# First weights of the output projection loaded and split under the branches' merge, and the gate block summed two column tiles sooner

## Chip, cores, metric

One core of a Trainium2 chip. The metric is the device time of one execution in microseconds (us); several executions give a median. Engine names are those of the profile: PE multiplies matrices (PEld loads its weights), DVE is the vector engine, ACT the scalar engine, POOL is GpSimd, SP is the queue that issues nearly all transfers.

## What is computed

One layer on 640 tokens (128 context, 512 latent) of width 1024. The change lies in the middle of it, where the two branches are projected, merged by gates, and projected once more:

```python
ga, gb = jnp.split(gates, 2, axis=-1)
m = jax.nn.sigmoid(ga) * y_a + jax.nn.sigmoid(gb) * y_b
return m @ w_out, ...
...
x = x + gt1 * rms_norm(y, norm_gains[1])
```

Here `y_a = o @ w_br_a` and `y_b = (...) @ w_br_b` are the branches' projections (512 to 1024 columns each), and `gt1` is one 1024-wide block of `mod = silu(c) @ w_mod + b_mod`, the "gate block" of the title.

## The kernel before

Every float32 operand is split into a high and a low part (`split`, L50: ACT casts the high part, line L57; DVE subtracts it, line L58), and each product is three matmuls (`mm3`, lines L83 to L85). Weights stream from memory into raw buffers (`wr`), are split into `wh` and `wl`, and go to PE as the stationary operand. PSUM tiles of the projections are named `d` and have three buffers.

The order of work on each engine comes from a scheduler that takes the program in the order in which it is written, with priorities. An engine takes its instructions strictly in that order, and so does the SP queue: a transfer that waits holds up those behind it.

The stages that matter here, in order:

- Gate projections: `gate_th(i)` loads a weight tile, multiplies by the layer's input `hT` (two tiles `hT0` and `hT1` of 20 KB a partition), ACT takes the tanh (L735), and the result goes to memory as `thd`. Between them stand the last short convolution (`short(3)`, its product with the third projection on DVE at L724, its result stored as `ybd`, L725) and the sums of two other blocks of `mod` (`cm_rows`: matmuls on L208 and L209, then a round trip through memory into `sc2`, which DVE waits for at L249).
- Merge: for each of 8 column tiles `j`, load `w_br[j]` and two `thd` tiles (`bth`), four half projections of 12 matmuls (branch b, then branch a), and DVE and ACT form the merged tile as `mh[:, j]` and `ml[:, j]`. The input `y_b` is first read back from `ybd` in one transfer of 1280 KB (tile `ybr`, L972) and split into `ybh` and `ybl`; `y_a` is split from `zf` into `yah` and `yal`. Raw weights come from the pool `bp` with five buffers, which the gate block's `w_mod` tiles share.
- Gate block: `row_job` (L196) adds each of 8 `w_mod` tiles into two accumulators `gacc` on DVE (16 operations of 128x1024), one tile per column tile `j`. After the eighth, each accumulator is split (`cph`, `cpl`), summed over partitions by PE (L208, L209), and multiplied into `gt1` (L225).
- Output projection: `w_out` comes in eight tiles of 512 KB through two raw buffers, is split into the pool `wo` (eight buffers each for `woh` and `wol`), and PE forms `acc` for each token tile: `some(range(3), 0)` for the first three, then `prod`. This stage's PE order is written out by hand.

Pools are stacked from both ends of SBUF. What a pool places where a closed pool lay must wait until the old tiles have been read for the last time. The right-hand pool `hp2` is opened after the pools of `hT` and of the convolutions' tiles are closed, and covers part of where `hT1` lay.

Of the kernel before, what the change touches and what calls it, by code (L numbers as in the profile page):

```python
# [9 lines left out]
F32 = mybir.dt.float32  # L10
# [8 lines left out]
P = 128  # L19
D = 1024  # L20
# [3 lines left out]
TOK = CTX + LAT  # L24
# [13 lines left out]
class Kernel:  # L38
# [700 lines left out]
    def run(self):  # L739
        nc, tc, I, O = self.nc, self.tc, self.I, self.O  # L740
        pool = lambda st, name, bufs=1, **kw: st.enter_context(
            tc.tile_pool(name=name, bufs=bufs, **({} if kw.get("space") == DRAM else {"reuse_waits": "tile"}), **kw))
        stack = lambda *a, **kw: (lambda st: (st, pool(st, *a, **kw)))(ExitStack())
# [8 lines left out]
        hst, hp = stack("hp", side="right")  # L752
# [134 lines left out]
        def scan(p):  # L887
            with tc.high_priority(offset=300000):
# [26 lines left out]
        rows2 = lambda p: [p.tile([P, D], F32, name="gacc", tag="gacc", bufs=2) for _ in range(2)]  # L915
        raws = lambda p, n: lambda: p.tile([P, D], F32, name="wr", tag="wr", bufs=n)
        fill = itertools.chain(*(self.row_job(blk, rows2(mb), raws(mb, 4), self.cm_rows(cm[n], mb, ma, parts))
                                 for blk, n in ((3, "sh2"), (4, "sc2"))))
# [28 lines left out]
        for _ in fill:  # L947
# [11 lines left out]
        fd = lambda: self.psd.tile([P, 512], F32, name="d", tag="d")  # L959
        hst, hp = stack("hp2", side="right")  # L960
        mst, mp = stack("mp", side="right")
        gst, gp = stack("gp", side="right")
        b0st, bp0 = stack("bp0")
        bst, bp = stack("bp")
        self.rpool, self.nraw = bp, 5
        gt1 = gp.tile([P, 2, D], F32, name="gt1")
        fill = self.row_job(2, rows2(bp0), raws(bp, 5), self.gate_rows(gt1, 1, bp0.tile([P, D], F32, name="grow"), fd,
                                                                lambda acc: self.split(acc, [P, D], "cp", bp0, 1, urgent=False)))
        mh = mp.tile([P, KT, TOK], F32R, name="mh")
        ml = mp.tile([P, KT, TOK], F32R, name="ml")  # L970
        ybr = bp.tile([P, 4, TOK], F32, name="ybr")
        nc.sync.dma_start(out=ybr, in_=self.ybd.rearrange("i p t -> p i t"))  # L972
        yb = self.split(ybr, [P, 4, TOK], "yb", bp, 1)
        ya = self.split(self.zf, [P, 4, TOK], "ya", bp, 1)
        for j in range(KT):
            wb = self.load_w(I["w_br"][j], [P, 8, P])
            th = []
            for n in range(2):
                t_ = bp0.tile([P, TOK], F32, name="bth", tag="bth", bufs=4)
                nc.sync.dma_start(out=t_, in_=self.thd[2 * j + n])  # L980
                th.append(t_)
            for n, y in ((1, yb), (0, ya)):
                for h in range(2):
                    s = slice(h * HALF, (h + 1) * HALF)
                    ps = self.gemm_cm([w_[:, 4 * n:4 * n + 4, :] for w_ in wb], y, h, 4)
                    with self.urgent():
                        nc.vector.scalar_tensor_tensor(out=th[n][:, s], in0=th[n][:, s], scalar=1.0, in1=ps,
                                                       op0=ALU.add, op1=ALU.mult)
            next(fill, None)
            m = th[1]  # L990
            with self.urgent():
                nc.vector.tensor_tensor(out=m, in0=th[0], in1=th[1], op=ALU.add)
                nc.scalar.copy(out=mh[:, j, :], in_=m)
                nc.vector.tensor_tensor(out=ml[:, j, :], in0=m, in1=mh[:, j, :].bitcast(F32), op=ALU.subtract)
# [2 lines left out]
            pass  # L997
        bst.close()
        b0st.close()
        self.rpool, self.nraw = self.wpool, 2  # L1000

        wst2, wf = stack("wf", 2)
        pools = itertools.cycle((wf, self.wpool))
        h2 = [mh, ml]
        yst, bp = stack("yp", side="right")
        wost, wo = stack("wo")
# [4 lines left out]
        def load_o(src):  # L1013
            raw = self.rpool.tile([P, 2, 512], F32, name="wr", tag="wr", bufs=self.nraw)
            nc.sync.dma_start(out=raw, in_=src)
            return self.split(raw, [P, 2, 512], "wo", wo, 8)
        ws = [[load_o(I["w_out"][h, kk]) for kk in range(4)] for h in range(2)]
        ys = {}
        zx, xs = zp.tile([P, 4 * TOK], F32, name="zf"), {}
        quad = lambda: hp.tile([P, 4, TOK], F32, name="hq", tag="hq", bufs=2)  # L1020
        f = [quad(), quad()]

        def prod(t, h):
# [220 lines left out]
        with tc.manual_schedule(engines={mybir.EngineType.PE}):  # L1244
# [23 lines left out]
            for i, j in enumerate(rest):  # L1268
# [3 lines left out]
                if last:  # L1272
# [10 lines left out]
        fill = self.row_job(5, rows2(fq), raws(self.rpool, 2), self.gate_rows(gt2, 3, fq.tile([P, D], F32, name="grow2"), fd,  # L1283
                                                                      lambda acc: self.split(acc, [P, D], "w", next(pools), urgent=False)))
# [3 lines left out]
        def load_f(src):  # L1288
            raw = self.rpool.tile([P, 2, 512], F32, name="wr", tag="wr", bufs=self.nraw)
            nc.sync.dma_start(out=raw, in_=src)  # L1290
            return self.split(raw, [P, 2, 512], "w", next(pools))
# [22 lines left out]
        for kk in order:  # L1314
            split_act(kk)
            w = load_f(I["w_ffn_out"][0, kk])
# [10 lines left out]
        for kk in order[:-TAIL]:  # L1327
            if kk < NK - 6:
                split_act(kk)
            w = load_f(I["w_ffn_out"][1, kk])  # L1330
            for t in range(NT):
                part(acc[t], w, kk, t, order)
        ws = []
# [98 lines left out]
```

## Time and profile before

| what | value |
|---|---|
| median of 3 runs | 1089.17 us (1086.23 to 1091.02) |
| profiled execution, its own time | 1085.44 us |
| span of the profiled execution | 1083.7 us |
| PE busy | 1019.8 us, 94% of the span |
| DVE busy | 836.9 us, 77% |
| mean granted PE clock | 0.981 |

The span is what the profile shows of that execution; its own time also holds what lies around the span (1.7 us). Busy is time in which the engine executed. Matmuls are pipelined, so a matmul's duration in a row is longer than its step from start to start.

### The profile page before, as it was taken

To read this page: it belongs to the slowest core of one execution; us is meant where nothing else is said; L and a number is where in the kernel's file an instruction comes from. 1 tells how busy PE (TensorE), PEld (TensorE's weight loads), DVE (VectorE), ACT (ScalarE), POOL (GpSimd) and SP (SyncE) were. 2 spreads that over 40 slices of the span, in tenths; PEclk is the share of its full clock that TensorE was granted. 3 is DMA by queue.
4 is the path that set the end of the run, shared out by engine and by line. 5 is a ranking of instruction groups with operands and counts; after the bars stand their busy time and mean duration, and the time that the engine had idled before them with its cause. 6 is when DMAs were issued, how large, how long until landed. Compare 5 with 4: busy or idle time off the path is not lost.

```text
span 1083.7 us, 19694 instructions
## 1 busy us (share of the span) xinstructions
PE 1019.8 (94%) x7729; PEld 925.9 (85%) x7729; DVE 836.9 (77%) x1698; ACT 483.2 (45%) x927; POOL 141.9 (13%) x168
## 2 busy tenths in 40 slices
PE   6999988988988989999998998999999999999997
PEld 3699987878887788899996887999999999788885
DVE  5767997897898888895895789888777775975336
ACT  5568436415525323434223476444445444624321
POOL 2215321153063050101000000000000000000000
PEclk9999989998999999999999998999999999999999
DMA  9335712163282374557853532323222322552214
GB/s 346 144 91 136 205 60 75 57 138 107 62 188 89 99 179 166 173 166 241 309 183 116 180 113 88 104 86 98 93 79 78 98 83 74 176 171 99 79 39 156
DMA packets 47399, 141.52 MB, mean 131 GB/s; under 512 B 9517, under 2 KB 10034, under 8 KB 47306
## 3 DMA queue, kind: packets, MB, share of 16 engines
q1 hardware_dynamic: 42746, 127.10, 35.9%
q0 software_dynamic: 4560, 13.15, 5.6%
q8 instruction: 61, 1.00, 0.4%
q14 instruction: 32, 0.26, 0.1%
HBM read 117.57 MB, written 12.18 MB: 120 GB/s over the span
## 4 chain that ended last, share of the span: by engine, by line
PE 63%; DVE 18%; DMA 3%; ACT 2%; issue 2%; SPq 1%; POOL 0%; DVEq 0%; ACTq 0%; POOLq 0%
PE acc L1166 21%; PE d L85 6%; PE d L83 6%; PE d L84 6%; PE acc L84 5%; PE acc L83 5%; PE acc L85 5%; PE d L1166 3%; DVE X L561 3%; DVE otmp L559 2%; PE s L643 2%; DVE wl L58 2%; PE v L614 1%; PE v L673 1%; DVE RT L565 1%
## 5 line engine op out<-in xcount | busy, mean ns | idle before, releaser
L83 PE MATMUL d<-hT,wh 128*128 128x320 f32 x720 | 228.4, 318 | 1.8 <-DVE cy L724 1.8
L85 PE MATMUL d<-hT,wl 128*128 128x320 f32 x720 | 228.9, 318 | 0.4 <-DVE wl L58 0.4
L84 PE MATMUL d<-hT,wh 128*128 128x320 f32 x720 | 227.2, 316 | 0.0
L57 ACT CAST wh<-wr 128x512 fp32r<-128x512 f32 x150 | 88.1, 620 | 155.1 <-PE d L84 90.4
L83 PEld LDWEIGHTS d<-hT,wh 128*128 128x128 f32 x720 | 137.3, 191 | 4.3 <-DVE cy L724 2.1
L85 PEld LDWEIGHTS d<-hT,wl 128*128 128x128 f32 x720 | 137.3, 191 | 4.2 <-issue 1.2
L84 PEld LDWEIGHTS d<-hT,wh 128*128 128x128 f32 x720 | 137.5, 191 | 2.0 <-issue 0.3
L58 DVE TENSOR_TENSOR wl<-wr,wh 128x512 fp32r<-128x512 f32 x150 | 103.1, 709 | 44.3 <-ACT wh L57 43.5
L1166 PE MATMUL acc<-mh,wl 128*128 128x320 f32 x280 | 86.9, 310 | 1.8 <-DVE wl L1101 1.8
L83 PE MATMUL acc<-wh,as 128*128 128x512 f32 x220 | 85.7, 390 | 2.1 <-ACT as L1300 2.1
L1166 PE MATMUL acc<-mh,wh 128*128 128x320 f32 x280 | 87.0, 311 | 0.3 <-ACT early L1180 0.3
L1166 PE MATMUL acc<-ml,wh 128*128 128x320 f32 x280 | 86.7, 310 | 0.0
L84 PE MATMUL acc<-wl,as 128*128 128x512 f32 x220 | 85.6, 389 | 0.0
L85 PE MATMUL acc<-wh,as 128*128 128x512 f32 x220 | 85.5, 389 | 0.0
L196 DVE SCALAR_TENSOR_TENSOR gacc<-wr,cv,gacc 128x1024 f32<-128x1024 f32 x64 | 80.7, 1280 | 4.0 <-DMA wr<-in_w_mod_dram 3.7
L1105 ACT CAST wh<-wr 128x512 fp32r<-128x512 f32 x66 | 40.7, 623 | 71.6 <-PE acc L1166 36.9
L1105 ACT CAST wh<-S 128x512 fp32r<-128x512 f32 x88 | 54.3, 621 | 36.3 <-PE d L1166 19.6
L1101 DVE TENSOR_TENSOR wl<-S,wh 128x512 fp32r<-128x512 f32 x88 | 60.2, 688 | 3.8 <-ACT wh L1105 2.9
L1101 DVE TENSOR_TENSOR wl<-wr,wh 128x512 fp32r<-128x512 f32 x66 | 45.4, 690 | 19.1 <-ACT wh L1105 18.1
L1166 PEld LDWEIGHTS acc<-mh,wl 128*128 128x128 f32 x280 | 52.8, 189 | 2.1 <-DVE wl L1101 2.0
L1166 PEld LDWEIGHTS acc<-mh,wh 128*128 128x128 f32 x280 | 52.7, 188 | 0.6 <-ACT early L1180 0.6
L1166 PEld LDWEIGHTS acc<-ml,wh 128*128 128x128 f32 x280 | 52.8, 189 | 0.0
(365 smaller groups left out, 2344.0 us busy)
## 6 DMA issues: line engine op xcount, KB each, us to landing
wr<-in_w_ffn_in_dram SPq DMA_DIRECT2D x48, 512.0 KB
wr<-in_w_in_dram SPq DMA_DIRECT2D x45, 512.0 KB
wr<-in_w_mod_dram SPq DMA_DIRECT2D x32, 512.0 KB
wr<-in_w_ffn_out_dram SPq DMA_DIRECT2D x22, 512.0 KB
mr<-in_w_mod_dram SPq DMA_DIRECT2D x16, 512.0 KB
thd<-gt SPq DMA_DIRECT2D x16, 320.0 KB
bth<-thd SPq DMA_DIRECT2D x16, 320.0 KB
wr<-in_w_br_dram SPq DMA_DIRECT2D x8, 512.0 KB
```

The costliest lines, as they stand in the source:

```text
L57: (high or nc.scalar.copy)(out=hi[:, s], in_=raw[:, s])
L58: (low or nc.vector).tensor_tensor(out=lo[:, s], in0=raw[:, s], in1=hi[:, s].bitcast(F32), op=ALU.subtract)
L83: mm(out, lhsT=ah, rhs=bh, start=start, stop=False)
L84: mm(out, lhsT=ah, rhs=bl, start=False, stop=False)
L85: mm(out, lhsT=al, rhs=bh, start=False, stop=stop)
L196: nc.vector.scalar_tensor_tensor(out=acc[v], in0=w, scalar=self.cv[:, k, v:v + 1], in1=acc[v], op0=ALU.mult, op1=ALU.add)
L559: nc.vector.tensor_tensor(out=t, in0=B[:, j + 1:32, j:j + 1].broadcast_to([P, n, j]), in1=X[:, j:j + 1, 0:j].broadcast_to([P, n, j]), op=A ...
L561: nc.vector.tensor_tensor(out=X[:, j + 1:32, 0:j], in0=X[:, j + 1:32, 0:j], in1=t, op=ALU.subtract)
L643: mm(ps[half(c2), o:o + 64], lhsT=w(d, c2, t, hd), rhs=R[:, d, c2, t, hd, :], start=True, stop=True)
L1101: tt = lambda o, a, b, op: nc.vector.tensor_tensor(out=o, in0=a, in1=b, op=op)
L1105: nc.scalar.copy(out=dst[0], in_=src)
L1166: nc.tensor.matmul(ps, lhsT=A[x][:, k], rhs=B[y][:, k], start=start and k == 0 and n == 0, stop=k == 3 and n == 2, skip_group_check=True)
```

## The change

It opens the pool `wf` (which before was opened after the merge) ahead of the merge's pools, lets two `w_out` tiles be loaded and split into it at `j` = 4 and 5, and cuts the pool `wo` from eight to six buffers. The `w_br` tiles of the merge now go through the two raw buffers of `wpool`; the gate block has three raw buffers of its own. Its first four `w_mod` tiles are taken two per column tile, so that its sums are written out at `j` = 5. The tile that takes `y_b` is moved from `bp` to the pool `hp2` (tag `hq`).

```diff
+        wst2, wf = stack("wf", 2)
         b0st, bp0 = stack("bp0")
         bst, bp = stack("bp")
-        self.rpool, self.nraw = bp, 5
         gt1 = gp.tile([P, 2, D], F32, name="gt1")
-        fill = self.row_job(2, rows2(bp0), raws(bp, 5), self.gate_rows(gt1, 1, ...
+        fill = self.row_job(2, rows2(bp0), raws(bp, 3), self.gate_rows(gt1, 1, ...
...
-        ybr = bp.tile([P, 4, TOK], F32, name="ybr")
+        quad = lambda: hp.tile([P, 4, TOK], F32, name="hq", tag="hq", bufs=2)
+        ybr = quad()
         nc.sync.dma_start(out=ybr, in_=self.ybd.rearrange("i p t -> p i t"))
...
+        ws0 = []
         for j in range(KT):
...
-            next(fill, None)
+            for _ in range(2 if j < 2 else 1):
+                next(fill, None)
+            if j in (4, 5):
+                raw = self.wpool.tile([P, 2, 512], F32, name="wr", tag="wr")
+                nc.sync.dma_start(out=raw, in_=I["w_out"][0, j - 4])
+                ws0.append(self.split(raw, [P, 2, 512], "w", wf))
...
-        self.rpool, self.nraw = self.wpool, 2
-        wst2, wf = stack("wf", 2)
...
-            return self.split(raw, [P, 2, 512], "wo", wo, 8)
-        ws = [[load_o(I["w_out"][h, kk]) for kk in range(4)] for h in range(2)]
+            return self.split(raw, [P, 2, 512], "wo", wo, 6)
+        ws = [ws0 + [load_o(I["w_out"][0, kk]) for kk in (2, 3)], [load_o(I["w_out"][1, kk]) for kk in range(4)]]
```

How the change moves instructions is shown at three places. Lines behind the edit are numbered some five higher after the change.

First the SP queue where the gate projections end. `ybr`, after the change `hq`, is the tile that takes `y_b`; `thd<-gt` are the stores of the last gate projections; `in_w_br` and `in_w_mod` are weights of the merge and of the gate block. Before:

```order
L725 DMA ybd<-cy 128x640 [waits DMAHW5_49,DVE_49]
L216 DMA grow<-in_gains_row_dram 128x1024 [waits DMAHW6_49,Activation_49]
L736 DMA thd<-gt 128x640 [waits Activation_49]
L972 DMA ybr<-ybd 128x4x640 [waits DMASW6_49,DMASW4_49,DMASW7_49,DMASW2_49,DMAHW0_49,DMASW1_49,DMAHW5_49,DMASW0_49,PE_49]
L63 DMA wr<-in_w_br_dram 128x1024 [waits DMAHW1_49]
L736 DMA thd<-gt 128x640 [waits Activation_49]
```

After:

```order
L194 DMA wr<-in_w_mod_dram 128x1024 [waits DMAHW1_49,DVE_49]
L194 DMA wr<-in_w_mod_dram 128x1024 [waits DMAHW2_49,DVE_49]
L736 DMA thd<-gt 128x640 [waits DMAHW3_49,Activation_49]
L63 DMA wr<-in_w_br_dram 128x1024 [waits DMAHW4_49,DVE_49]
L194 DMA wr<-in_w_mod_dram 128x1024 [waits DMAHW7_49,DMAHW5_49]
L973 DMA hq<-ybd 128x4x640 [waits DMAHW6_49,PE_49]
```

The read of `y_b` stood behind the first of four last stores of `thd` and ahead of all weights of the merge; now it stands behind the last of these stores, behind the fourth `w_br` tile and behind the seventh `w_mod` tile. What the waits stand for is read from the built program's semaphore counts: the `PE_49` of `ybr` was a gate-sum matmul of another block (the last L209 on `m`), the `PE_49` of `hq` is the last but one matmul of the last gate projection, since `hq` lies where `hT1` lay. The `DVE_49` of the `w_br` tile is the second half of the split of the `w_br` tile two before it (`j` = 1), and that split in turn waits for the last but one matmul of the last gate projection, whose weight buffers it takes over.

Next DVE from there to the merge's first products (L987, after the change L989). `yal` and `ybl` are the low parts of `y_a` and `y_b`, `s_86` is the scale that waits for `sc2`. Before:

```order
L724 TENSOR_TENSOR cy<-cy,d 128x320
L58 TENSOR_TENSOR wl<-wr,wh 128x512 x2
L58 TENSOR_TENSOR yal<-zf,yah 128x1280 x2
L249 SCALAR_TENSOR_TENSOR s_86<-sc_84,gains 128x16
L58 TENSOR_TENSOR wl<-wr,wh 128x512 x2
L58 TENSOR_TENSOR ybl<-ybr,ybh 128x1280 x2
L58 TENSOR_TENSOR wl<-wr,wh 128x512 x2
L196 SCALAR_TENSOR_TENSOR gacc<-wr,cv,gacc 128x1024 x2
L58 TENSOR_TENSOR wl<-wr,wh 128x512 x2
L987 SCALAR_TENSOR_TENSOR bth<-bth,d 128x320
```

After:

```order
L724 TENSOR_TENSOR cy<-cy,d 128x320
L58 TENSOR_TENSOR wl<-wr,wh 128x512 x2
L249 SCALAR_TENSOR_TENSOR s_86<-sc_84,gains 128x16
L58 TENSOR_TENSOR wl<-wr,wh 128x512 x2
L196 SCALAR_TENSOR_TENSOR gacc<-wr,cv,gacc 128x1024 x4
L58 TENSOR_TENSOR wl<-wr,wh 128x512 x2
L196 SCALAR_TENSOR_TENSOR gacc<-wr,cv,gacc 128x1024 x4
L58 TENSOR_TENSOR wl<-wr,wh 128x512 x2
L196 SCALAR_TENSOR_TENSOR gacc<-wr,cv,gacc 128x1024 x6
L58 TENSOR_TENSOR ybl<-hq,ybh 128x1280 x2
L196 SCALAR_TENSOR_TENSOR gacc<-wr,cv,gacc 128x1024 x2
L989 SCALAR_TENSOR_TENSOR bth<-bth,d 128x320 x2
```

All 16 additions of the gate block now stand ahead of the merge's first product, 14 of them ahead of the split of `y_b`; before, 14 of the 16 stood in the merge. The split of `y_a` has gone further ahead, to before the last short convolution's product (L724).

Last PE where the gate block is summed. Before, at the end of the merge, `wo` being the output projection's weights:

```order
L85 MATMUL d<-yah,wl 128x320
L208 MATMUL d<-cph,onesr 128x512
L209 MATMUL d<-cpl,onesr 128x512
L208 MATMUL d<-cph,onesr 128x512
L209 MATMUL d<-cpl,onesr 128x512
L208 MATMUL d<-cph,onesr 128x512 x2
L209 MATMUL d<-cpl,onesr 128x512 x2
L83 MATMUL acc<-woh,mh 128x512
L84 MATMUL acc<-wol,mh 128x512
```

After, behind column tile 5:

```order
L85 MATMUL d<-yah,wl 128x320
L208 MATMUL d<-cph,onesr 128x512
L209 MATMUL d<-cpl,onesr 128x512
L208 MATMUL d<-cph,onesr 128x512
L209 MATMUL d<-cpl,onesr 128x512
L83 MATMUL acc<-wh,mh 128x512
L84 MATMUL acc<-wl,mh 128x512
L85 MATMUL acc<-wh,ml 128x512
L83 MATMUL acc<-wh,mh 128x512
L208 MATMUL d<-cph,onesr 128x512
L84 MATMUL acc<-wl,mh 128x512
L208 MATMUL d<-cph,onesr 128x512
```

The eight sums have moved two column tiles forward, and matmuls of the output projection (15 of them on the two early weight tiles, 21 more at the end of the merge) now stand between and behind them.

## Rows read from the trace of the kernel before

**Rows 1.** The page: span; busy us with its share of the span, by engine.

```profile
span 1083.7 us, 19694 instructions
...
PE 1019.8 (94%) x7729; PEld 925.9 (85%) x7729; DVE 836.9 (77%) x1698; ACT 483.2 (45%) x927; POOL 141.9 (13%) x168
```

**Rows 2.** Windows of 20 us: busy us by engine, clock, DMA share, GB/s.

```profile
core 0: us, PE busy (x) PEld busy (x) DVE busy (x) ACT busy (x) POOL busy (x), PEclk, DMA share, GB/s
...
500.00:520.00 20.00, 20.00 (x139) 20.00 (x138) 11.78 (x15) 7.61 (x13) 0.00 (x0) 1.00 0.83 278
...
540.00:560.00 20.00, 20.00 (x139) 20.00 (x138) 19.59 (x30) 6.04 (x11) 0.00 (x0) 1.00 0.71 247
560.00:580.00 20.00, 16.75 (x94) 14.58 (x94) 16.40 (x27) 5.35 (x9) 0.00 (x0) 0.95 0.11 34
580.00:600.00 20.00, 20.00 (x85) 16.28 (x85) 9.43 (x16) 8.51 (x18) 0.00 (x0) 0.96 0.53 177
```

**Rows 3.** Timeline of PE, 490 to 516 us: start, duration, operation, idle time before.

```profile
490.75 0.31 PE L83 MATMUL d<-hT,wh 128*128 128x320 f32 x1
...
515.24 0.31 PE L85 MATMUL d<-hT,wl 128*128 128x320 f32 x1
515.38 0.30 PE L83 MATMUL d<-ybh,wh 128*128 128x320 f32 x1
```

**Rows 4.** Timeline of PE, 571 to 582 us, where the merge ends.

```profile
571.70 0.39 PE L208 MATMUL d<-cph,onesr 128*128 128x512 f32 x1
571.93 0.39 PE L209 MATMUL d<-cpl,onesr 128*128 128x512 f32 x1
...
575.04 0.49 PE L209 MATMUL d<-cpl,onesr 128*128 128x512 f32 x1 [0.76 <-DVE cpl L58]
576.38 0.50 PE L209 MATMUL d<-cpl,onesr 128*128 128x512 f32 x1 [0.84 <-DVE cpl L58]
...
578.25 0.80 PE L84 MATMUL acc<-wol,mh 128*128 128x512 f32 x1 [1.15 <-DVE wol L58]
578.85 0.63 PE L85 MATMUL acc<-woh,ml 128*128 128x512 f32 x1
579.27 0.63 PE L83 MATMUL acc<-woh,mh 128*128 128x512 f32 x1
...
581.68 0.39 PE L83 MATMUL acc<-woh,mh 128*128 128x512 f32 x1
```

**Rows 5.** Timeline of the SP queue, 496 to 580 us.

```profile
496.39 0.39 SPq L972 DMA_DIRECT2D ybr<-ybd  x1
...
516.78 0.44 SPq L63 DMA_DIRECT2D wr<-in_w_br_dram  x1
...
579.43 13.97 SPq L1015 DMA_DIRECT2D wr<-in_w_out_dram  x6
```

**Rows 6.** Timeline of ACT, 503 to 584 us.

```profile
503.07 2.44 ACT L57 CAST ybh<-ybr 128x1280 fp32r<-128x1280 f32 x2 [0.20 <-DMA ybr<-ybd]
...
515.44 0.62 ACT L57 CAST wh<-wr 128x512 fp32r<-128x512 f32 x1 [2.88 <-PE d L84]
...
583.04 2.41 ACT L57 CAST woh<-wr 128x512 fp32r<-128x512 f32 x4 [5.11 <-DMA wr<-in_w_out_dram]
```

**Rows 7.** Timeline of DVE, 480 to 518 us.

```profile
480.15 3.67 DVE L196 SCALAR_TENSOR_TENSOR gacc<-wr,cv,gacc 128x1024 f32<-128x1024 f32 x3
...
488.31 0.48 DVE L724 TENSOR_TENSOR cy<-cy,d 128x320 f32<-128x320 f32 x1
...
496.98 2.89 DVE L58 TENSOR_TENSOR yal<-zf,yah 128x1280 fp32r<-128x1280 f32 x2 [0.47 <-ACT yah L57]
502.85 0.17 DVE L249 SCALAR_TENSOR_TENSOR s<-sc,gains 128x16 f32<-128x16 f32 x1 [2.98 <-DMA sc<-cscr]
...
504.37 2.89 DVE L58 TENSOR_TENSOR ybl<-ybr,ybh 128x1280 fp32r<-128x1280 f32 x2
...
516.94 0.69 DVE L58 TENSOR_TENSOR wl<-wr,wh 128x512 fp32r<-128x512 f32 x1 [0.15 <-ACT wh L57]
```

More of the change, by code (lines that the diff above doesn't have):

```diff
@@ L962, in run @@
         gst, gp = stack("gp", side="right")
+        wst2, wf = stack("wf", 2)
         b0st, bp0 = stack("bp0")
         bst, bp = stack("bp")
-        self.rpool, self.nraw = bp, 5
         gt1 = gp.tile([P, 2, D], F32, name="gt1")
-        fill = self.row_job(2, rows2(bp0), raws(bp, 5), self.gate_rows(gt1, 1, bp0.tile([P, D], F32, name="grow"), fd,
+        fill = self.row_job(2, rows2(bp0), raws(bp, 3), self.gate_rows(gt1, 1, bp0.tile([P, D], F32, name="grow"), fd,
                                                                 lambda acc: self.split(acc, [P, D], "cp", bp0, 1, urgent=False)))
@@ L1015, in load_o @@
             nc.sync.dma_start(out=raw, in_=src)
-            return self.split(raw, [P, 2, 512], "wo", wo, 8)
-        ws = [[load_o(I["w_out"][h, kk]) for kk in range(4)] for h in range(2)]
+            return self.split(raw, [P, 2, 512], "wo", wo, 6)
+        ws = [ws0 + [load_o(I["w_out"][0, kk]) for kk in (2, 3)], [load_o(I["w_out"][1, kk]) for kk in range(4)]]
         ys = {}
         zx, xs = zp.tile([P, 4 * TOK], F32, name="zf"), {}
-        quad = lambda: hp.tile([P, 4, TOK], F32, name="hq", tag="hq", bufs=2)
         f = [quad(), quad()]
```

## The prediction

> **What bounds the kernel now.** I read the page first: PE is busy in 94% of the span, DVE in 77%, so a change pays where PE stands still or slows, and costs where it makes PE wait [rows 1]. Then the windows: from 500 to 560 us, under the last gate projections and the merge, PE is busy all the time at full clock, and at 560 to 580 it is not, at a clock of 0.95 [rows 2]. Then PE's timeline there. The merge's matmuls run without a gap from 515.38 to 571.70, 384 of them at 0.147 us [rows 3, 4]. At 571.70 the gate block's sums begin. The reader should see that PE waits for ACT and DVE three times there, and that from 578.25 to 581.68 the steps are 0.42 us instead of 0.23: the clock is at half [rows 4]. Eight sums and nine products of the output projection take 9.98 us, and 17 x 0.23 = 3.94 would do. So **6.0 us** can be had, and nothing else in the stretch that the change touches: elsewhere in the merge PE is full.
>
> **The merge's end.** The sums move under column tiles 6 and 7, and two tiles of `w_out` lie split when the merge ends. The waits at 575.04 and 576.38 and that for `wol` at 578.25 have then other matmuls to cover them, and the half clock behind them, which alone costs 3.43 - 8 x 0.23 = 1.6 us for eight matmuls, has no cause. What I leave: the order puts the sums close behind the split of the accumulators again, with 0.84 us for one wait there before [rows 4]; I take 0.6 for what is not covered (0 to 1.6). The other tiles of `w_out` still come through two raw buffers, and before a first cast behind such a load came 3.6 us after its issue (579.43 to 583.04) [rows 5, 6]; here 36 matmuls of prepared work (15 and 21, 8.4 us) cover it, and I take 0.5 for the tiles of the second half (0 to 2). Together -6.0 + 0.6 + 0.5 = **-4.9 us** (-6 to -3).
>
> **What is free.** The number of matmuls and of vector operations stays the same. Sixteen `gacc` additions at 1.2 us (three take 3.67) are 19.2 us of DVE [rows 7]; they go into the tail of the gate projections, where DVE is busy for 11.78 of 20 us, and leave the merge, where it was busy for 19.59 of 20 [rows 2]. Relief of DVE there gains nothing, since PE was full. The `w_br` tiles go through two raw buffers instead of five; a column tile takes 48 x 0.147 = 7.0 us, a load some 3.6, so it stays hidden. Where that cover is gone it costs 3.6 for each tile late.
>
> **Reading `y_b` back.** This is the large term. Before, the read was issued at 496.39 and `ybh` was cast from 503.07, 0.20 after the data came: 6.5 us from issue to landing, all of it 12 us ahead of the merge's first matmul at T = 515.38 [rows 3, 5, 6]. After the change the tile lies where `hT1` was, so it may only be written when PE has read `hT1` for the last time, one matmul before T. And the order shows it in the SP queue behind the `w_br` tile of `j` = 3, which waits for the split of the tile of `j` = 1. That split waits for PE's last gate projection in its turn: before, ACT's cast of such a tile stood waiting for PE until 515.44, and DVE's second half ended at 516.94 + 0.69, T + 2.25 [rows 6, 7]. Everything behind the waiting issue is held, `y_b` among it, and for `y_b` the merge's first product waits. Step by step: T + 2.25, two issues ahead of it at 0.44 and the gaps between them [rows 5], so T + 3.4. Landing 7.0 later (6.5 measured at a quieter time; weights issued just ahead share the way here; 5.5 to 8): T + 10.4. The cast of the first half 0.2 later, 1.2 long (`ybh` took 2.44 for two halves): T + 11.8. Then two subtractions of 1.45 (2.89 for two): the second `ybl` at T + 14.7 [rows 6, 7]. By then PE can do 11 of the merge's matmuls, those that need only high parts, the first half, or `y_a` (1.6 us). The `gacc` additions that stand ahead of `ybl` on DVE (six, 7.2 us from T + 2.25) end at T + 9.5, before `ybh` is there. The wait is thus 14.7 - 1.6 = **+13.1 us** (11.5 with a landing at 5.5; 15 with one at 8 and a queue held a little longer).
>
> The Trainium skill (SBUF — State Buffer, "The DMA setup-cost knee") gives a transfer a fixed 2 us and then the bytes at up to 436 GB/s. For 1.31 MB that would be an estimate of 5.0 us, and the sum would come out 2 us lower, at 1099.0; the row has 6.5 for this very transfer, so I stay with the row.
>
> **The clock behind that wait.** After a standstill PE comes back slow: behind waits of 0.8 to 1.15 us close together it ran 3.4 us at half clock and lost 1.6 us [rows 4]. Behind one of 10 us and more I take the same, **+1.5 us** (0.5 if the matmuls that trickle in between the halves already bring it back, 3 if it takes twice as long).
>
> The Trainium skill (TensorE: Matmul & The Clock Gate, "HAM oscillation — how this bites in real kernels") says the same of a kernel in which PE waits for a DMA: each burst behind the wait starts cold. It speaks against this change, which makes such a wait; the trace bears it out with its 0.95 and 0.96 around 578 us.
>
> **The split of `y_a`, moved ahead.** The order has it now before the last convolution's product (L724), which frees the PSUM buffer that PE's next projection takes. That product began at 488.31 with no idle time before it, and PE's next group at 490.75 [rows 3, 7]. Ahead of it come two subtractions of 1.45, and a weight half and a `cpl` of some 0.6 each: 4.1 us. It would end at 488.31 + 0.48 + 4.1 = 492.9, 2.1 after PE wants the buffer: **+2.1 us** (0 if the scheduler's other moves absorb it, 4 if nothing does). The round trip into `sc2`, for which DVE waits 2.98 us until 502.85, starts that much later too; its user (L249) is needed only near T, so it costs nothing unless it slips by more than some 8 us.
>
> **Sum.** -4.9 + 13.1 + 1.5 + 2.1 = +11.8 us. On the profiled execution's 1085.44 that is 1097.2; the median of the runs lies 3.73 higher, so **1101.0 us**. By the bounds, taken all low or all high, +6 to +19; these rarely fall together, so 1095 to 1107 is the forecast's own range.
>
> **The rivals.**
>
> *The wait is shorter.* Without the queue's hold-up `y_b` goes at T + 0.5, 2.9 sooner; with a landing of 5.5, 1.5 sooner; with the early `y_a` free, 2.1 less; with a clock that costs 0.5, 1 less. All four: 11.8 - 7.5 = +4.3, 1093.5 us. For it: each of the four sizes rests on a single row. Against it: the order of SP is strict, and the row at 515.44 shows the cast that everything hangs on.
>
> *The wait is longer.* The four `thd` reads and the weight tiles are issued beside `y_b`; before, the DMA share at 500 to 520 was already 0.83 [rows 2]. A landing of 9 to 10 us and a second stall in the merge because `w_br` is late (3.6) make +16 to +20, 1107 to 1112.
>
> *The other side: the read of `y_b` is hidden.* If the tile can be written before the gate projections end, or the scheduler's matmuls of `y_a` go first, PE doesn't wait, and only the gain at the merge's end is left, -4.9 + 2.1 = -2.8, at best -6: 1083 to 1086 us. It decides by `y_b`'s halves being split within 2.8 us of T. Against it: from its issue to the cast alone were 6.5 us, and the first product of a column tile is the one with `y_b`. The tile would have to lie somewhere else than the wait on PE in the order says.
>
> *It doesn't do what it says:* the sums, though moved, wait as long as before and the early tiles change nothing. Then the -4.9 is lost and the sum is +16.7, 1106; it lies inside the range of the longer wait.
>
> **How the numbers follow.** The wait as worked out 0.66, the shorter one 0.17, the longer 0.10, hidden 0.07. What this kernel's measurement can tell from no change is about 0.5%, 5.4 us: 1083.8 to 1094.6. Faster needs the hidden wait with nearly all of the gain: 0.05. The rest of that case, and most of the shorter wait, fall within: 0.16. Slower: 0.79. The range of 8 in 10 leaves out the hidden case and part of the longer one: 1092.5 to 1109.
>
> **What the profile after would show.** Right: PE idle for some 11 to 13 us in one to three pieces at the start of the merge, released by ACT's `ybh` and DVE's `ybl`, ACT in its turn by the DMA into `hq`, whose issue stands 3 us behind the last gate projection; a granted clock well under 1 in that window; no waits of 0.8 us and more among the gate sums, and the first `acc` matmul right behind the last `yah` one; a wait of about 2 us on `d` near 491. Wrong: an `hq` issue before the last projection, a landing under 4 us, or a wait at the merge's end that stays, with PE held by `woh` or `wol` of the second half.

## The result and the profile after

The changed kernel takes **1102.05 us** (median of 6 runs, 1098.66 to 1108.42), the kernel before 1089.12 (6 runs, 1086.23 to 1091.02). The ratio is **1.0131**, 95% interval 1.0106 to 1.0156: 12.9 us slower. The forecast was 1101.0, range 1092.5 to 1109.

The page after, with the span and the busy times:

```profile
span 1106.7 us, 19708 instructions
...
PE 1026.5 (93%) x7729; PEld 931.0 (84%) x7729; DVE 840.7 (76%) x1698; ACT 482.6 (44%) x927; POOL 142.1 (13%) x168
```

The profiled execution is the slowest of the six (1108.42 us), so its span can't be set against [rows 1] as it is. Matched matmul by matmul, it is 8.25 us late already at 470 us of before's trace, in stages where both programs have the same order: a difference between executions. At 725 us of before it is 22.96 late, and stays so to the end (the spans differ by 23.0). The change's own part is thus 22.96 - 8.25 = **14.7 us**, all of it between the last convolution and the first token tiles of the output projection. It rests on one execution of each kernel.

The windows (columns as in [rows 2]; T, the end of the gate projections, lies at 527.36 here, one step of 0.15 behind the start of their last matmul):

```profile
500.00:520.00 20.00, 19.32 (x119) 19.00 (x120) 9.15 (x15) 5.17 (x11) 4.23 (x5) 0.91 0.59 193
520.00:540.00 20.00, 7.53 (x52) 7.26 (x50) 15.40 (x15) 3.94 (x8) 0.00 (x0) 0.81 0.81 285
540.00:560.00 20.00, 19.26 (x115) 19.03 (x116) 14.78 (x22) 6.43 (x10) 0.00 (x0) 0.85 0.19 61
```

Where PE was full at clock 1.00 before, it now has 7.53 busy us of 20, at 0.81, and the next window is at 0.85. PE's timeline has the rest: first the other blocks' sums, then the first merge matmuls.

```profile
498.52 0.40 PE L208 MATMUL m<-cph,onesr 128*1 128x512 f32 x1 [0.36 <-ACT cph L57]
499.30 0.40 PE L209 MATMUL m<-cpl,onesr 128*1 128x512 f32 x1 [0.38 <-DVE cpl L58]
500.68 0.40 PE L209 MATMUL m<-cpl,onesr 128*1 128x512 f32 x1 [0.76 <-DVE cpl L58]
...
501.68 0.47 PE L83 MATMUL d<-hT,wh 128*128 128x320 f32 x1
...
540.74 0.90 PE L83 MATMUL d<-ybh,wh 128*128 128x320 f32 x2 [13.21 <-ACT ybh L57]
...
545.36 0.47 PE L84 MATMUL d<-ybl,wh 128*128 128x320 f32 x1
545.63 0.45 PE L85 MATMUL d<-ybh,wl 128*128 128x320 f32 x1
545.89 0.33 PE L83 MATMUL d<-ybh,wh 128*128 128x320 f32 x1
546.06 0.31 PE L84 MATMUL d<-ybl,wh 128*128 128x320 f32 x1
```

Three things are to be seen. At 498 to 501 PE waits three times, 1.5 us in all, for `cph` and `cpl` of the other blocks; with the slow steps around and behind these waits (0.27 us until 504.9) 3.7 us are lost, where before none were. At 540.74 it has waited 13.21 us for `ybh`. Then the steps are 0.27 us until 545.89, and 0.15 from there on: the half clock (1.2 GHz of 2.4) lasts 5.1 us and costs 2.5.

The chain behind the long wait: SP's queue, then ACT, then DVE.

```profile
529.63 0.33 SPq L63 DMA_DIRECT2D wr<-in_w_br_dram  x1
...
530.53 0.39 SPq L973 DMA_DIRECT2D hq<-ybd  x1
```

```profile
527.42 0.62 ACT L57 CAST wh<-wr 128x512 fp32r<-128x512 f32 x1 [2.89 <-PE d L84]
...
539.43 2.42 ACT L57 CAST ybh<-hq 128x1280 fp32r<-128x1280 f32 x2 [10.55 <-DMA hq<-ybd]
```

```profile
528.26 1.34 DVE L58 TENSOR_TENSOR wl<-wr,wh 128x512 fp32r<-128x512 f32 x2
...
540.72 1.49 DVE L58 TENSOR_TENSOR ybl<-hq,ybh 128x1280 fp32r<-128x1280 f32 x1 [2.08 <-ACT ybh L57]
```

The cast of the `w_br` tile stands at T (527.42) as it did at 515.44 in [rows 6], its low part ends on DVE at 529.6, SP issues the next `w_br` tile at 529.63, and `hq` at 530.53, T + 3.2. The data are there just ahead of 539.43: 8.7 us from issue to landing, against 6.5 before [rows 5, 6].

The merge's end, which answers to [rows 4]; here it is a wait in the merge, then the eight sums and the first early products behind column tile 5:

```profile
577.65 0.41 PE L83 MATMUL d<-yah,wh 128*128 128x320 f32 x1 [0.78 <-DVE bth L989]
...
586.86 0.40 PE L208 MATMUL d<-cph,onesr 128*128 128x512 f32 x1
...
591.60 0.39 PE L85 MATMUL acc<-wh,ml 128*128 128x512 f32 x1
...
592.41 0.40 PE L209 MATMUL d<-cpl,onesr 128*128 128x512 f32 x1
...
592.94 0.40 PE L209 MATMUL d<-cpl,onesr 128*128 128x512 f32 x1
```

From 586.86 to 592.94 no row carries a wait; before, four waits (3.2 us; the fourth, for `cph`, stands in the rows of the first experiment) and a half clock stood there. New is the wait at 577.65, for a free buffer of `d`, which DVE empties (`bth`, L989).

### The profile page after: what moved, and what is told of

It is laid out like the page before. It is cut to its first block, busy times and chain, and to the rows that moved or that the text cites. A ratio compares the mean times of both kernels' runs of the same rounds, so it can differ in the third digit from the quotient of the medians.

```text
span 1106.7 us, 19708 instructions
## 1 busy us (share of the span) xinstructions
PE 1026.5 (93%) x7729; PEld 931.0 (84%) x7729; DVE 840.7 (76%) x1698; ACT 482.6 (44%) x927; POOL 142.1 (13%) x168
## 4 chain that ended last, share of the span: by engine, by line
PE 73%; DVE 17%; ACT 4%; issue 2%; DMA 2%; POOL 1%; SPq 0%; DVEq 0%; ACTq 0%; POOLq 0%
PE acc L1171 20%; PE d L83 8%; PE d L85 8%; PE d L84 8%; PE acc L83 6%; PE acc L85 6%; PE acc L84 6%; PE d L1171 3%; DVE otmp L559 3%; DVE X L561 2%; DVE wl L58 2%; PE s L643 2%; PE v L673 1%; ACT wh L57 1%; PE m L790 1%
## 5 line engine op out<-in xcount | busy, mean ns | idle before, releaser
L58 DVE TENSOR_TENSOR wl<-wr,wh 128x512 fp32r<-128x512 f32 x154 | 105.4, 706 | 51.3 <-ACT wh L57 50.4
L83 PEld LDWEIGHTS d<-hT,wh 128*128 128x128 f32 x720 | 138.9, 193 | 5.4 <-DVE cy L724 3.2
L84 PEld LDWEIGHTS d<-hT,wh 128*128 128x128 f32 x720 | 138.8, 193 | 2.2 <-issue 0.5
L1106 DVE TENSOR_TENSOR wl<-wr,wh 128x512 fp32r<-128x512 f32 x66 | 45.4, 688 | 15.9 <-ACT wh L1110 14.9
```

Of the source, the lines that this page charges most:

```text
L58: (low or nc.vector).tensor_tensor(out=lo[:, s], in0=raw[:, s], in1=hi[:, s].bitcast(F32), op=ALU.subtract)
L83: mm(out, lhsT=ah, rhs=bh, start=start, stop=False)
L84: mm(out, lhsT=ah, rhs=bl, start=False, stop=False)
L1106: tt = lambda o, a, b, op: nc.vector.tensor_tensor(out=o, in0=a, in1=b, op=op)
```

## Experiments

Each ratio is to the kernel before, run on the same chip; between experiments, ratios are compared, since the chips differ. "Own part" is how much later PE stands at 725 us of before's trace than at 470, as worked out above for the changed kernel (14.7 us); it leaves out what differs between executions elsewhere, and rests on one execution of each kernel.

**The tile alone.** The kernel before, and only the place of the tile changed:

```diff
+        quad = lambda: hp.tile([P, 4, TOK], F32, name="hq", tag="hq", bufs=2)
-        ybr = bp.tile([P, 4, TOK], F32, name="ybr")
+        ybr = quad()
```

> The kernel before with one edit: the tile that takes y_b is placed in hp2, over hT1. The order keeps the split of y_a behind the last convolution here, and the sums stay at the merge's end. Theory: the issue waits for the last gate projection and for the w_br tile ahead of it, PE idles 12 to 14 us, 2 to 3 us go to the half clock, and nothing is gained at the merge's end: 1102 to 1107 us. Rival, the wait comes from the early additions and loads of the whole change and not from the place of the tile: within 4 us of the kernel before.

Measured: 1105.43 us, ratio 1.016 (1.0128 to 1.0193), own part 17.3 us. PE's waits from 480 to 625 us (us in total, times, longest), and SP's and ACT's rows:

```profile
PE d L83 <- ACT ybh L57: 14.6, 1, 14.6
PE d L209 <- DVE cpl L58: 1.6, 2, 0.8
PE acc L84 <- DVE wol L58: 1.0, 1, 1.0
PE d L208 <- ACT cph L57: 0.5, 1, 0.5
```

```profile
524.73 0.33 SPq L63 DMA_DIRECT2D wr<-in_w_br_dram  x1
525.15 0.39 SPq L973 DMA_DIRECT2D hq<-ybd  x1
```

```profile
534.04 2.42 ACT L57 CAST ybh<-hq 128x1280 fp32r<-128x1280 f32 x2 [11.94 <-DMA hq<-ybd]
```

The four small waits of the merge's end are those of before (the one for `cph` is the fourth wait there, which [rows 4] leave out); the 14.6 us are new, and half clock behind them costs 2.0. The issue stands at T + 4.6 here (T is 520.6), and issue to landing is again 8.7 us (525.15 to just ahead of 534.04). By the own parts this one placement costs 2.6 us more than the whole change, and everything else in the change gives that back; the intervals of the two ratios overlap.

**The tile out of the way.** The changed kernel, `y_b` read in two halves through a buffer outside `hT1` (its cast and subtraction by halves, as `split` does them):

```diff
-        fill = self.row_job(2, rows2(bp0), raws(bp, 3), ...
+        fill = self.row_job(2, rows2(bp0), raws(bp, 2), ...
-        ybr = quad()
+        for i in (0, 2):
+            ybr = bp.tile([P, 2, TOK], F32, name="ybr", tag="ybr", bufs=1)
+            nc.sync.dma_start(out=ybr, in_=self.ybd[i:i + 2]...)
```

> The changed kernel, but y_b is read back in two halves through one buffer of 5 KB a partition in the pool bp, which does not lie where hT1 lay (one raw buffer of the gate block is given up for the space). If the wait for y_b is the loss (theory: 13.4 us of idle PE and about 2.5 us of half clock, both seen in the trace after), PE goes from the last gate projection into the merge without a gap, the gain at the merge's end stays, and the time is 1085 to 1091 us. Rival 1, the loss only changes place (the weights through two raw buffers or the gate block's additions come late instead): PE idles 5 us or more elsewhere in the merge and the time is 1095 us or more. Rival 2, the end of the merge gained nothing: 1091 to 1095 us.

Measured: 1093.35 us, ratio 1.0054 (1.0031 to 1.0076), own part 3.1 us. PE runs into the merge without a gap, so the 13 us are the wait for `y_b`; yet the time is above the theory's range and within that of rival 2. That rival doesn't hold by the trace, since the own part is smaller than the loss that stands ahead of the merge, at the other blocks' sums, where the first half of `y_b` is now split early as well. PE's first matmul of the merge, and its waits from 480 to 525 us:

```profile
525.08 0.30 PE L83 MATMUL d<-ybh,wh 128*128 128x320 f32 x1
```

```profile
PE m L208 <- ACT cph L57: 2.1, 3, 0.9
PE m L209 <- DVE cpl L58: 1.5, 3, 0.8
```

Three and three waits, with the slow steps 6.2 us lost where the changed kernel lost 3.7. DVE had 1.45 us more to do ahead of these sums. From the merge on, this kernel is thus 3.1 us faster than the kernel before (own part 3.1 less 6.2).

**Another queue.** `y_b`'s read in the changed kernel issued with `nc.gpsimd` for `nc.sync`.

> The changed kernel, with the read of y_b issued by GpSimd's queue and not by SP's, so that it no longer stands behind the w_br tile. Theory: the issue moves from 3.2 us to under 1 us behind the last gate projection and the wait shrinks by 2 to 3 us, 1098 to 1101 us. Rival, the landing is set by the traffic of the tiles issued beside it: the wait stays at 13 us, 1101 to 1104 us, or GpSimd's own issue takes longer and the time is above that.

Measured: 1105.72 us, ratio 1.0164 (1.0137 to 1.019). The issue did move to the end of the gate projections, and PE still lost more. GpSimd's row, PE's waits, and DVE:

```profile
518.22 0.77 POOL L973 DMA_DIRECT2D hq<-ybd  x1 [15.95 <-PE d L85]
```

```profile
PE d L83 <- ACT ybh L57: 11.8, 1, 11.8
PE d L84 <- DVE ybl L58: 4.0, 1, 4.0
```

```profile
530.03 4.87 DVE L196 SCALAR_TENSOR_TENSOR gacc<-wr,cv,gacc 128x1024 f32<-128x1024 f32 x4 [4.56 <-DMA wr<-in_w_mod_dram]
534.82 2.89 DVE L58 TENSOR_TENSOR ybl<-hq,ybh 128x1280 fp32r<-128x1280 f32 x2
```

The cast began at 528.60, so the landing took 10.2 us from its issue: three microseconds sooner in the queue, and 1.4 sooner at PE. Then a second wait opened: `ybl` stood on DVE behind four additions whose `w_mod` tile had not come. The theory failed: what the queue gave, the longer landing took back in part, and the second wait more than the rest. Whether the landing was longer for the queue or for the loads beside it, the run doesn't tell.

**The split of `y_a`, with less priority.** In the changed kernel `ya = self.split(..., urgent=False)`.

> The changed kernel, with the split of y_a given no priority over what is written ahead of it; the order then has its first half behind the first steps of the last convolution. Theory: PE's waits of 2.6 us on L724's product between 490 and 503 us come from these two subtractions, and 1.5 to 3 us of them go, so 1099 to 1100.5 us. Rival, the additions of the sums (gacc) that stand ahead of L724 make that wait: the waits stay and the time is that of the changed kernel, 1102 us.

Measured: 1102.6 us, ratio 1.0136 (1.0107 to 1.0166).

```profile
PE d L83 <- ACT ybh L57: 14.1, 1, 14.1
PE d L83 <- DVE cy L724: 2.0, 1, 2.0
```

The order still had both halves ahead of L724's product, and the wait went there (2.0 us): the edit did not do what it was meant to, and tells nothing of the cause. The expectation also took PE's waits in the changed kernel for waits on L724's product; its rows show them at the sums, for `cph` and `cpl`.

**The split of `y_a`, held behind.** The changed kernel with a copy of two elements, which the split overwrites:

```diff
+        nc.vector.tensor_copy(out=ya[0][:, 0:4:2, 0:1], in_=cm["sc2"][:, 0:2, 0:1])
```

> The changed kernel, with the split of y_a held behind the first value of sc2 by a copy of two elements a partition into yah (overwritten by the split), so that both halves stand behind the last convolution on DVE, as in the kernel before. Theory: the 3.7 us that PE loses among the other blocks' sums and behind them (waits of 2 us, half clock 1.6 us) go, the wait for y_b stays: 1097.5 to 1100 us. Rival, the other moved work (weight splits, additions) makes those waits: they stay and the time is that of the changed kernel, 1102 us.

Measured: 1103.93 us, ratio 1.0138 (1.0115 to 1.0162), own part 13.4 us. The loss between 490 and 503 us is gone altogether, as the theory had it; and the wait for `y_b` has grown to 16.3 us, so that the time is above the theory's range. PE's only wait from 480 to 625 us, then DVE and SP, with T at 516.83:

```profile
PE d L83 <- ACT ybh L57: 16.3, 1, 16.3
```

```profile
512.96 4.99 DVE L196 SCALAR_TENSOR_TENSOR gacc<-wr,cv,gacc 128x1024 f32<-128x1024 f32 x4
517.87 0.68 DVE L58 TENSOR_TENSOR wl<-wr,wh 128x512 fp32r<-128x512 f32 x1
519.81 1.28 DVE L196 SCALAR_TENSOR_TENSOR gacc<-wr,cv,gacc 128x1024 f32<-128x1024 f32 x1 [1.26 <-DMA wr<-in_w_mod_dram]
521.01 0.68 DVE L58 TENSOR_TENSOR wl<-wr,wh 128x512 fp32r<-128x512 f32 x1
```

```profile
521.72 0.34 SPq L63 DMA_DIRECT2D wr<-in_w_br_dram  x1
...
523.34 0.39 SPq L973 DMA_DIRECT2D hq<-ybd  x1
```

Four additions now stand ahead of the `w_br` split on DVE, its second half waits behind one more, whose tile came late, and ends at 521.7. SP's next issue is at 521.72, `hq` at T + 6.5. The 3 us saved ahead of T were spent behind it.

**Sums alone.** The kernel before with `for _ in range(2 if j < 2 else 1): next(fill, None)` and nothing else.

> The kernel before, with one edit: the gate block's first four w_mod tiles are taken two for each column tile, so that its sums stand behind column tile 5; nothing is moved in memory and no w_out tile is split early. Theory: of the 6.0 us lost at the merge's end the waits for cpl (and the half clock behind them) go and the wait for the first wol stays, so 2 to 4 us are gained: 1085 to 1087 us. Rival: the sums wait as long behind column tile 5 as they did at the end, no change, 1088 to 1090 us.

Measured: 1094.34 us, ratio 1.0061 (1.0038 to 1.0083): slower, which neither theory had. PE's waits:

```profile
PE acc L83 <- ACT woh L57: 3.7, 1, 3.7
PE d L209 <- DVE cpl L58: 3.7, 2, 2.9
```

Behind column tile 5 the sums wait for `cpl` for 3.7 us, longer than at the end (1.6). And the merge's end, without the sums, waits 3.7 us for the first `woh`. With the slow steps, counted from PE's timeline, some 7 us are lost at each of the two places, against 6.0 in all before. So the sums at the end were not only a loss: PE did them while ACT and DVE split the first weights.

**Without the early tiles of `w_out`.** The small-buffer kernel with all eight `w_out` tiles loaded behind the merge and `wo` at eight buffers.

> The kernel of the run with the small buffer, without the two early tiles of w_out (all eight come behind the merge into a pool of eight buffers again), with the sums behind column tile 5 as in the change. Theory: with the sums gone from the merge's end nothing covers the split of the first tile of w_out, and PE waits 4 to 5 us for woh and wol there, so 2 to 4 us above the small buffer's run: 1095 to 1098 us. Rival: the early tiles aren't what pays, and the time is that of the small buffer's run, 1093 us.

Measured: 1098.14 us, ratio 1.0082 (1.0054 to 1.011), against 1.0054 with them.

```profile
PE acc L83 <- ACT woh L57: 2.7, 1, 2.7
PE d L83 <- DVE gt L225: 1.8, 1, 1.8
PE d L208 <- ACT cph L57: 0.7, 1, 0.7
```

The wait for `woh` is back, as the theory had it, but its 2.7 us are less than the 4 to 5 expected; the time lies at the upper end of the theory's range. The ratio is 0.28% higher, 3 us, and the intervals overlap; the own parts (10.9 and 3.1) differ by 7.8. Counted from PE's steps, with half clock, 6.2 us are lost at the merge's end against 2.6 in the small buffer's run, and 6.1 against 1.2 around the sums, where early products no longer stand between them and a wait of 1.8 us for the product into `gt1` (L225) is new. So the trace shows what the early tiles cover, and the timed runs leave open how much it is worth.

**The tenants exchanged.** In the changed kernel `y_b` is read into `bp`, and the eight `w_mod` tiles go through the two tiles `hq`; `y_a` held back as above.

> The changed kernel, with the two tenants exchanged: y_b is read into the pool bp, and the gate block's w_mod tiles take the two tiles hq over hT1, since they are needed later than y_b; the split of y_a held back as in the run beside. Theory: both losses ahead of the merge go, no idle PE from 490 us into the merge, and what is left is the gain at the merge's end, 2 to 5 us: 1083 to 1087 us. Rival, the w_mod tiles, loaded after the last gate projection through two buffers, make the gate block's sums late and PE waits for them near the merge's end: 1088 to 1095 us.

Measured: 1097.13 us, ratio 1.0092 (1.0064 to 1.012). The rival's mechanism held, at a time above its range: nothing is lost from 490 us into the merge, but the sums wait 7.1 us for additions whose tiles were loaded only behind T. PE had done all 36 early products of `w_out` ahead of these late sums, and at the merge's end, with none left to cover it, it waits for the first `woh` again.

```profile
PE d L208 <- ACT cph L57: 7.1, 1, 7.1
PE acc L83 <- ACT woh L57: 2.7, 1, 2.7
```

**Both splits held back.** The small-buffer kernel, with the copy above for `y_a` and one like it for the first half of `y_b`.

> The kernel of the run with the small buffer, with the splits of y_a and of the first half of y_b held behind the first value of sc2, so that none of them stands ahead of the last convolution. Theory: the 6.2 us that PE lost there among the other blocks' sums go, nothing else changes, and the merge's end keeps its gain of 2 to 4 us: 1084.5 to 1087.5 us, faster than the kernel before by up to 0.4%. Rival: y_b's second half comes too late for the merge's first product, or the weights' splits do, and PE waits there: 1088 us or more.

Measured: 1088.59 us (12 runs), ratio 0.9999 (0.9983 to 1.0016), own part -2.7 us. The 6.2 us ahead of the merge are gone; against the small buffer's run that is 0.55%, about the 6 us.

```profile
PE acc L84 <- DVE wol L58: 0.7, 3, 0.2
PE d L208 <- ACT cph L57: 0.7, 1, 0.7
```

What is left are these waits, 1.4 us, none of them the rival's, though the time is in its range and above the theory's. The own part says faster, the timed runs say equal, with an interval down to -1.9 us; why they differ stays open.

**Sums one step apart.** That kernel, with eight tiles taken in the first four column tiles and the sums written out at `j` = 6, one step behind the last addition:

```diff
-            if k < KT - 1:
+            if late or k < KT - 1:
                 yield
...
-            for _ in range(2 if j < 2 else 1):
+            for _ in range(2 if j < 4 else j == 6):
```

> The kernel of the run beside, with the gate block's eight tiles taken two for each of the first four column tiles and its sums one step apart from the last addition, behind column tile 6. Theory: the sums no longer wait for the split of the accumulators (1 us and less in the small buffer's run), so 0 to 1.5 us below the run beside. Rival: the order moves and PE waits elsewhere, within 1 us of it or above.

Measured: **1084.44 us** (11 runs, 1079.07 to 1087.61), ratio **0.9957** (0.9941 to 0.9974): faster than the kernel before by 0.4%. Its own part is -3.1 us. The gain over the run beside, 4 us in the medians, is more than expected; by the own parts it is 0.4, so the traces don't show where most of it comes from.

```profile
PE d L83 <- DVE bth L999: 1.3, 3, 0.6
PE d L208 <- DVE bth L999: 0.5, 1, 0.5
```

PE no longer waits for `cph`, `cpl`, `woh` or `wol`; what is left are waits of 0.6 us and less for a free `d`.

## Why the prediction was right, step by step

**Reading `y_b` back**, +13.1: measured 13.2, and 14.6 with the tile alone. The mechanism is as told: the tile lies over `hT1`, and the issue stands behind the `w_br` tile that waits in its turn (T + 3.2, forecast T + 3.4). Inside, two sizes were off and cancelled, which is luck. The landing took 8.7 us, above the forecast's bound of 8; and PE started on the first `ybh` at T + 13.4, not held by `ybl` afterwards, because at half clock the matmuls that need only high parts or `y_a` lasted until `ybl` came. The Trainium skill (SBUF — State Buffer, "The DMA setup-cost knee") gave an estimate of 5.0 us for this transfer; the trace, with weights beside it on the way, has 8.7 in two kernels, and decides. That those weights make the difference is argued and not shown.

**The clock**, +1.5: measured 2.5, 5.1 us of half clock behind the wait: the mechanism as told, its size 1.0 us too small. The Trainium skill (TensorE: Matmul & The Clock Gate, "HAM oscillation — how this bites in real kernels") says that the work behind such a wait starts cold; the windows at 0.81 and 0.85 agree.

**The split of `y_a` ahead**, +2.1: measured 3.7 as a loss at that place. The cause is shown (held behind, the loss is 0). The place was another, so here the mechanism was only half right: PE waited at the other blocks' sums, for `cph` and `cpl`, and not for L724's product, and a stretch of half clock came on top. But the step treats it as a term by itself, and the same run shows that it wasn't: without it the wait for `y_b` grew by 3 us, since the work on DVE that had been late ahead of T was then late behind it.

**The merge's end**, -4.9: what is left of the own part is 14.7 - 3.7 - 13.2 - 2.5 = -4.7. Counted from PE's steps, 6.0 us were lost before and some 1.5 are now, which makes about -4.5. The rest isn't where the forecast left it: nothing is lost at the sums and at the tiles of the second half (0.6 and 0.5 forecast), and most of the 1.5 stands behind the wait of 0.78 us for a free `d`. The forecast said why only in half: it took the sums' waits for a plain loss. The run with the sums alone shows that they covered the first split of `w_out`, and that moving them alone doesn't gain. Early tiles with the sums left at the end were not run, so what those gain alone is open.

**What is free**: the 16 additions were booked at nothing, hidden in the tail of the gate projections. In the changed kernel 14 of them end before or during the wait for `y_b`. With the wait gone they stand in the merge, and the sums wait 0.7 us for the split behind the last of them until they are spaced (the last two runs).

**The sum**, +11.8: the timed medians differ by 12.9, the own part is 14.7. The split of `y_a` and the clock came out 1.6 and 1.0 us above the forecast, and nothing inside the sum makes up for that; that 1101.0 lies within 1.1 us of the measured median is thus in part luck. Why the own part is above the difference of the medians stays open.

Of the rivals, the shorter wait was tested from its queue's side and fell; a hidden wait needs another place for the tile, and then the time came to 1093.35, to 1088.59 with the splits ahead of T held back, and only with the sums spaced to 1084.44, where that rival had put it. The longer wait's times were added up wrongly: +16 to +20 on 1089.17 are 1105 to 1109, not 1107 to 1112. Its landing of 9 to 10 us came nearly (8.7), its second stall did not.

## What to carry to other kernels

Where a tile takes the place of one that is still read, ask when that last read is, and whether the new tenant is needed right behind it: move there what is needed late, and count its whole chain (queue, landing, cast, subtraction) from the last read. A wait is paid for by what is done in it: taking one away exposes the work that it covered, so an edit that looks like a gain at one wait should be tried with its neighbour and alone. Work that a scheduler pulls ahead on a busy engine makes late whatever stands behind it there.

## What the runs showed of the hardware

The same transfer of 1280 KB took 6.5 us from issue to landing in the kernel before, 8.7 in two kernels that issue it among the merge's weights, and 10.2 from GpSimd's queue, whose issue took 0.77 us where SP's took 0.39; no run separates the loads beside it from the queue. Behind a standstill of 13.2 us PE ran 5.1 us in steps of 0.27 us before it came back to 0.15. Half clock followed much shorter waits too: behind 0.36, 0.38 and 0.76 us between 498 and 501 the steps were 0.27 us until 504.9.
